# A decoder layer on one core: one of the feed-forward operands is split again from its fp32 rows instead of being stored as two halves

## The chip, the cores and the metric

One of the eight cores of a Trainium2 chip runs the whole layer as one program. The metric is the device time of one execution in microseconds (us); lower is better. The engines are named as the profile names them: PE is TensorE, ACT is ScalarE, DVE is VectorE, POOL is GpSimd, SP is SyncE.

## What is computed

The reference is one hybrid decoder layer on a sequence of 2048 rows of 1024 fp32 values (`h`), with DEPTH 1:

```
u   = h @ W_in                                   # q | k | v | rnn-x | rnn-gate
att = sliding_window_sink_attention(q, k, v)     # 8 heads of 64, window 128
rec = rg_lru(causal_dwconv(rnn-x)) * gelu(rnn-gate)
mix = concat(att, rec) @ W_out
h   = LN1(alpha*h + mix)
ffn = (gelu(causal_dwconv(gate)) * val) @ w_down     with  gate | val = h @ w_up
ple = sigmoid(h @ W_g + b_g) * (p @ W_p)
h   = LN2(alpha*h + ffn + ple)
```

All matrix products are wanted to nearly fp32 accuracy.

## The kernel before

**Three products for one.** Each fp32 operand is split into two values that TensorE takes in one pass: a high half (ACT copies the fp32 tile to the type fp32r, line 122) and a low half (DVE subtracts the high half from the fp32 tile, line 123). This is `split_sb`. A product is then three matmuls, high by high, high by low, low by high (`mm3`, lines 140 to 142). So every weight block that SP loads (`wraw`, L132, into one of three `wst` buffers) passes through ACT and DVE before PE can take it.

**The first half of the layer, four chunks.** A loop `c` = 0 to 3 goes over chunks of 512 rows. In each it does the input projection, the recurrent branch, attention, the output projection and LN1, and then transposes the normalised rows with PE (L567). ACT and DVE make three things of each transposed tile: the halves `hh_[u]` and `hl_[u]` that the gate of the per-layer embedding needs at once, and the unsplit fp32 copy `hf[u]`. The index `u` = 0 or 1 names the first or the second 512 of the 1024 features. POOL then stores to DRAM what the feed-forward part will need: `hf[0]` and `hf[1]` (L573), and some of the split halves (L576). Behind these stores in POOL's queue, or ahead of them, stand the two loads of the next chunk's input (`xs`, L325). After that the chunk does the embedding's projection (`pps`, L596 copies its PSUM result out) and its gate (`gated`), each in two column halves `dh`. For `dh` = 1 the weights are loaded anew by SP.

**The second half, two pairs of chunks.** The feed-forward product `h @ w_up` is done for two chunks at a time (`s2` = 0 for chunks 0 and 1, `s2` = 1 for 2 and 3) with Strassen's seven products for eight. The operand's four quarters are B11 (features half 0, first chunk of the pair), B12 (half 0, second chunk), B21 (half 1, first chunk) and B22 (half 1, second chunk). B11, B21 and B22 are also used unsummed, in products of their own; the sums are T1 = B12 - B11, T3 = B22 - B12, T2 = T3 + B11 and T4 = B21 - T2. Before, the split halves of B11, B21 and B22 go to DRAM in the first half (`hxd`) and come back as they are (`load_split`, L258 and L261). The sums are made in `combine` from the fp32 rows that `stage` fetches with POOL (L239): for each of four k-tiles `kt`, B11 and B12 go into the two buffers of the ring `xb`, B22 into `xd`, B21 into `pch` or `pcl`. `combine` makes the sums on DVE (L279, L280, L282, L285) and splits T1 to T3 with `operand`, one ACT cast and one DVE subtract each. For pair 0 this runs while chunk 3's gate is computed, for pair 1 while the down-projection of chunk 1 runs.

**What sets the order.** The tile framework's scheduler orders the instructions of each engine when the program is built, by program order and by what it thinks is ready; each engine and each DMA queue then runs its list in order. PE's list is fixed by hand in `up` alone. The big tiles (operands, halves, `hf`, `xs`) share 13 slots of one ring, `h`; a tile waits there for the last reader of the slot's tile before it, a storing DMA included.

Of the kernel before, what the change touches and what calls it, by code (L numbers as in the profile page):

```python
# [8 lines left out]
F32 = mybir.dt.float32  # L9
# [6 lines left out]
P = 128  # L16
T = 512
# [17 lines left out]
def f(ap):  # L35
    return ap.bitcast(F32)
# [3 lines left out]
def kernel(  # L40
# [13 lines left out]
    ACT, DVE, POOL, PE, SP = nc.scalar, nc.vector, nc.gpsimd, nc.tensor, nc.sync  # L54
# [27 lines left out]
    def tm(tag, dt=F32, cols=512):  # L82
        return tmp.tile([P, cols], dt, tag=tag, name=nm(tag), bufs=BUFS.get(tag, 2))

    def h8(name, shape, dt=F32R):

        return h_p.tile(shape, dt, tag="h", name=nm(name))
# [15 lines left out]
    def order(i, earlier):  # L103
        for e in earlier:
            tc.add_manual_dep(
                i.ins, e.ins.name,
                mybir.DependencyInfo(mybir.DependencyClass.NoSync, mybir.DependencyReason.DATA),
                reason="issue order")
        return i
# [11 lines left out]
    def split_sb(src, hi, lo, eng=None):  # L121
        ACT.copy(hi, src)  # L122
        (eng or DVE).tensor_tensor(lo, src, f(hi), ALU.subtract)  # L123
# [73 lines left out]
    def scratch(name, shape, dt):  # L197
        return dr.tile(shape, dt, tag=name, name=name)

    rsd = [scratch(f"rsd{i}", [P, DM], F32) for i in range(NCH * NTOK)]  # L200
    hfd = [[scratch(f"hf{c}_{u}", [P, 4, T], F32) for u in range(2)] for c in range(NCH)]
    hxd = [{n: [scratch(f"hx{n}_{s}_{m}", [P, 4, T], F32) for m in range(2)] for n in ("B11", "B21", "B22")}
           for s in range(2)]
    gd = [[scratch(f"gd{s}_{k}", [P, 4, 2 * T], F32) for k in range(NF // 4)] for s in range(2)]

# [30 lines left out]
    hx = [{}, {}]  # L236
# [5 lines left out]
    def operands(s2, names):  # L242
        for n in names:
            hx[s2][n] = [[t[:, k, :] for k in range(4)] for t in (h8(n, [P, 4, T]), h8(n, [P, 4, T]))]

    def operand(s2, n, kt, src):
        split_sb(src, hx[s2][n][0][kt], hx[s2][n][1][kt])
# [3 lines left out]
    def load_split(s2, n, earlier):  # L251

        hx[s2][n] = []
        for m in range(2):
            if (n, m) == ("B22", 1):
                ts = [tm(("pch", "pcl")[k % 2], F32R) for k in range(4)]
                for k in range(4):
                    order(POOL.dma_start(f(ts[k]), hxd[s2][n][m][:, k, :]), earlier)  # L258
            else:
                t = h8(n, [P, 4, T])  # L260
                order(POOL.dma_start(f(t), hxd[s2][n][m]), earlier)  # L261
                ts = [t[:, k, :] for k in range(4)]
            hx[s2][n].append(ts)
# [8 lines left out]
    def combine(s2, kt):  # L272

        if kt == 0:
            load_split(s2, "B11", ())
            operands(s2, ("T2", "T1", "T3"))
        b11, b12, b22, b21 = staged[kt]
        t3, t1, t2 = (tm("xc") for _ in range(3))
        DVE.tensor_tensor(t3, b22, b12, ALU.subtract)  # L279
        DVE.tensor_tensor(t2, t3, b11, ALU.add)  # L280
        operand(s2, "T2", kt, t2)
        DVE.tensor_tensor(t1, b12, b11, ALU.subtract)  # L282
        operand(s2, "T1", kt, t1)
        operand(s2, "T3", kt, t3)
        DVE.tensor_tensor(b21, b21, t2, ALU.subtract)  # L285
# [6 lines left out]
    for c in range(NCH):  # L292

        def t_pair(name):
            return [[h8(name + m, [P, 4, T]) for _ in range(2)] for m in "hl"]
# [117 lines left out]
        for j in range(4):  # L413
            a, s, xc = rts[j][:, 0, :], rts[j][:, 1, :], xcs[j]
# [144 lines left out]
        hh_, hl_ = t_pair("h")  # L559
# [11 lines left out]

        for u in range(2):
            POOL.dma_start(hfd[c][u], hf[u])  # L573
        for u in range(c % 2, 2):
            for m, t in enumerate((hh_[u], hl_[u])):
                POOL.dma_start(hxd[c // 2][("B11", "B21", None, "B22")[2 * (c % 2) + u]][m], f(t))  # L576


        fence()
# [6 lines left out]
        for dh in range(2):  # L586
# [12 lines left out]
            for t_ in range(NTOK):  # L599
                ts_ = slice(t_ * P, (t_ + 1) * P)  # L600
                acc = bank("acc")
                for k in range(8):
                    b = ws[k // 2][k % 2]
                    gated = mm3(acc, hh_[k // 4][:, k % 4, ts_], hl_[k // 4][:, k % 4, ts_],
                        b[:, 0, :], b[:, 1, :], k == 0, k == 7)
                sg = tm("P")
                DVE.tensor_tensor(sg, acc, bg[:, ds_], ALU.add)
                act(sg, sg, AF.Sigmoid)
                DVE.tensor_tensor(sg, sg, pps[t_], ALU.mult)
                d = rs[t_][:, ds_]  # L610
                DVE.scalar_tensor_tensor(d, d, ALPHA, sg, ALU.mult, ALU.add)
                if dh == 1:
                    POOL.dma_start(rsd[c * NTOK + t_], rs[t_])
                if c == NCH - 1:
                    i = 4 * dh + t_
                    if i % 2 == 0:
                        stage(0, i // 2, last_scores)
                    else:
                        combine(0, i // 2)
# [108 lines left out]
    def down(s2):  # L728
# [5 lines left out]
        for ch in range(2):  # L734
# [32 lines left out]
            for kp in range(NF // 2 - 2):  # L767
                for dh in range(2):
                    wb = wunit(W_DOWN + 12 * dh + kp)
                    for t_ in range(NTOK):  # L770
                        i = sums(kp, t_, dh, gb, wb)
                    if dh == 0:
                        marks.append(i)
                gb = gated_pair(kp + 1)
                if later:
                    later.pop(0)()
                if c == 1 and 2 < kp < 7:
                    stage(1, kp - 3, marks[-1:])
                if c == 1 and 3 < kp < 8:
                    combine(1, kp - 4)  # L780
                if kp == NF // 4:
                    for t_ in range(NTOK):
                        rt = tm("r", cols=DM)
                        POOL.dma_start(rt, rsd[c * NTOK + t_])
                        rs.append(rt)
# [101 lines left out]
```

## Time and profile before

| | us |
|---|---|
| median of 3 runs | 2334.41 |
| lowest and highest of them | 2331.52 and 2335.72 |
| the profiled execution's own time | 2334.86 |
| its span, first to last instruction | 2333.2 |
| outside the span | 1.66 |

The profile is of one execution. A group line gives line, engine, operation and tiles, then count, busy time and mean duration. A line of a timeline gives start and duration in us, engine, line, operation and tiles and, in brackets, how long the engine sat idle before it and who released it. Matmuls are pipelined, so the distance between two starts, not the duration shown, is what one costs. In views by window the column PEclk is the granted TensorE clock as a share of full speed, and the DMA columns are the mean busy share of the 16 DMA engines and the GB/s that they moved.

### The profile page before, as it was taken

How to read it: one execution, taken by the hardware profiler on the slowest of the kernel's cores; microseconds unless marked ns; L12 is line 12 of the kernel's file. 1: busy time of each engine (PE TensorE's matmuls, PEld its weight loads, DVE VectorE, ACT ScalarE, POOL GpSimd, SP SyncE). 2: the span in 40 equal slices, each digit the busy share in tenths (PEclk: the TensorE clock that was granted, in tenths of full speed). 3: DMA queues.
4: the chain of work that ended last, by engine and by line, in shares of the span. 5: the costliest groups of instructions: out<-in, count | busy, mean ns of one | idle time of the engine just before them, and what ended most of it. 6: DMA issues, size and time to landing. Idle time of an engine off the chain costs nothing.

```text
span 2333.2 us, 28422 instructions
## 1 busy us (share of the span) xinstructions
PE 2279.2 (98%) x10156; PEld 1865.8 (80%) x10156; DVE 1654.2 (71%) x2728; ACT 1089.5 (47%) x2034; POOL 254.6 (11%) x477
## 2 busy tenths in 40 slices
PE   9998999999999999999999999999999999999998
PEld 7777877877787777888888888888888888888887
DVE  7975797678668888777777743768777777753735
ACT  7644674466456564444444433344544444433321
POOL 0311140013002311100000000010000000000000
PEclk9999999999999999999999999999999999999999
DMA  5336424532633465222222354664322222254642
GB/s 164 100 96 239 142 66 161 209 109 79 236 131 105 145 234 185 83 85 89 83 82 82 127 180 153 253 207 167 110 87 89 82 82 82 82 203 149 215 148 79
DMA packets 94638, 314.93 MB, mean 135 GB/s; under 512 B 9888, under 2 KB 10016, under 8 KB 89888
## 3 DMA queue, kind: packets, MB, share of 16 engines
q1 hardware_dynamic: 79200, 239.70, 31.1%
q0 software_dynamic: 15296, 73.41, 8.4%
q8 instruction: 80, 1.31, 0.2%
q14 instruction: 62, 0.51, 0.1%
HBM read 250.16 MB, written 62.91 MB: 134 GB/s over the span
## 4 chain that ended last, share of the span: by engine, by line
PE 59%; DVE 1%; DMA 0%; issue 0%; POOL 0%; DVEq 0%; POOLq 0%
PE b L140 7%; PE b L142 7%; PE b L141 7%; PE acc L142 5%; PE a L142 5%; PE a L140 5%; PE acc L140 5%; PE a L141 5%; PE acc L141 5%; PE sc L142 2%; PE sc L140 2%; PE sc L141 2%; DMA wst<-in_w_dram 0%; DVE st L214 0%; DVE r L798 0%; DVE r L220 0%
## 5 line engine op out<-in xcount | busy, mean ns | idle before, releaser
L122 ACT CAST wb<-wst 128x512 fp32r<-128x512 f32 x640 | 393.0, 622 | 672.9 <-PE acc L142 326.3
L123 DVE TENSOR_TENSOR wb<-wst,wb 128x512 fp32r<-128x512 f32 x640 | 434.2, 685 | 271.9 <-ACT wb L122 271.3
L140 PE MATMUL b<-T,wb 128*128 128x512 f32 x576 | 224.6, 390 | 1.6 <-DVE xd L686 0.8
L142 PE MATMUL b<-T,wb 128*128 128x512 f32 x576 | 224.1, 389 | 0.0
L141 PE MATMUL b<-T,wb 128*128 128x512 f32 x576 | 224.1, 389 | 0.0
L122 ACT CAST wb<-xc 128x512 fp32r<-128x512 f32 x144 | 89.3, 620 | 190.6 <-PE a L142 92.5
L141 PE MATMUL a<-B,wb 128*128 128x512 f32 x384 | 149.5, 389 | 0.1
L140 PE MATMUL a<-B,wb 128*128 128x512 f32 x384 | 149.4, 389 | 0.0
L142 PE MATMUL a<-B,wb 128*128 128x512 f32 x384 | 149.4, 389 | 0.0
L123 DVE TENSOR_TENSOR wb<-xc,wb 128x512 fp32r<-128x512 f32 x144 | 98.9, 687 | 49.2 <-ACT wb L122 49.2
L140 PEld LDWEIGHTS b<-T,wb 128*128 128x128 f32 x576 | 108.1, 188 | 25.7 <-DVE xd L686 1.9
L142 PEld LDWEIGHTS b<-T,wb 128*128 128x128 f32 x576 | 108.1, 188 | 22.5
L141 PEld LDWEIGHTS b<-T,wb 128*128 128x128 f32 x576 | 108.1, 188 | 22.4
L639 DVE SCALAR_TENSOR_TENSOR pl<-xb,prm,pl 128x512 f32<-128x512 f32 x96 | 71.8, 748 | 76.4 <-POOL xb L702 73.9
L142 PE MATMUL acc<-wb,hl 128*128 128x512 f32 x256 | 100.6, 393 | 1.7 <-DVE hl L98 1.7
L140 PE MATMUL a<-xh,wb 128*128 128x512 f32 x256 | 101.8, 398 | 0.0
L141 PE MATMUL a<-xl,wb 128*128 128x512 f32 x256 | 101.4, 396 | 0.0
L142 PE MATMUL a<-xh,wb 128*128 128x512 f32 x256 | 101.4, 396 | 0.0
L141 PE MATMUL acc<-wb,hh 128*128 128x512 f32 x256 | 100.5, 393 | 0.1
L140 PE MATMUL acc<-wb,hh 128*128 128x512 f32 x256 | 99.2, 393 | 1.0 <-ACT hh L97 1.0
L141 PEld LDWEIGHTS a<-B,wb 128*128 128x128 f32 x384 | 72.1, 188 | 15.5 <-DMA B<-hxB 0.5
L142 PEld LDWEIGHTS a<-B,wb 128*128 128x128 f32 x384 | 72.1, 188 | 14.9
(277 smaller groups left out, 5719.1 us busy)
## 6 DMA issues: line engine op xcount, KB each, us to landing
wst<-in_w_dram SPq DMA_DIRECT2D x319, 512.0 KB, 3.6
graw<-gd SPq DMA_DIRECT2D x24, 1024.0 KB, 6.4
gd<-pl SPq DMA_DIRECT2D x48, 256.0 KB, 2.0
gd<-r SPq DMA_DIRECT2D x48, 256.0 KB, 4.2
B<-hxB POOLq DMA_DIRECT2D x10, 1024.0 KB, 8.7
r<-in_xn_dram SPq DMA_DIRECT2D x16, 512.0 KB, 4.1
ln<-in_rows_dram POOLq DMA_DIRECT2D x16, 512.0 KB, 4.9
hf<-hf POOLq DMA_DIRECT2D x8, 1024.0 KB, 8.0
```

What stands on the lines that cost most here:

```text
L122: ACT.copy(hi, src)
L123: (eng or DVE).tensor_tensor(lo, src, f(hi), ALU.subtract)
L140: order(PE.matmul(o, ah, bh, start=first, stop=False, skip_group_check=more), after)
L141: PE.matmul(o, ah, bl, start=False, stop=False, skip_group_check=more)
L142: return PE.matmul(o, al, bh, start=False, stop=last, skip_group_check=more)
L639: DVE.scalar_tensor_tensor(gc, xb[:, t_:t_ + T], pc(C_FW + 3 * ft + t_), gc, ALU.mult, ALU.add)
```

## The change

The DRAM copies of B11's halves are gone, and with them their stores in chunks 0 and 2 (two of 1 MiB each per chunk) and their loads at the first step of `combine` (two of 1 MiB per pair). In their place `combine` treats B11 as it treats the sums: two tiles of the same ring `h` are taken by `operands`, and in each of its four steps `operand` splits the fp32 tile `b11`, which is fetched for the sums anyway. Per pair these are four ACT casts and four DVE subtracts of 128x512. The halves come out with the same values, because `hf` is the same PSUM tile that the stored halves were made from.

```diff
-    hxd = [{n: [scratch(f"hx{n}_{s}_{m}", [P, 4, T], F32) for m in range(2)] for n in ("B11", "B21", "B22")}
+    hxd = [{n: [scratch(f"hx{n}_{s}_{m}", [P, 4, T], F32) for m in range(2)] for n in ("B21", "B22")}
            for s in range(2)]
@@ def combine(s2, kt):
         if kt == 0:
-            load_split(s2, "B11", ())
-            operands(s2, ("T2", "T1", "T3"))
+            operands(s2, ("B11", "T2", "T1", "T3"))
         b11, b12, b22, b21 = staged[kt]
         t3, t1, t2 = (tm("xc") for _ in range(3))
         DVE.tensor_tensor(t3, b22, b12, ALU.subtract)
+        operand(s2, "B11", kt, b11)
         DVE.tensor_tensor(t2, t3, b11, ALU.add)
@@ for c in range(NCH):
         for u in range(2):
             POOL.dma_start(hfd[c][u], hf[u])
-        for u in range(c % 2, 2):
-            for m, t in enumerate((hh_[u], hl_[u])):
-                POOL.dma_start(hxd[c // 2][("B11", "B21", None, "B22")[2 * (c % 2) + u]][m], f(t))
+        for m, t in enumerate((hh_[1], hl_[1])):
+            POOL.dma_start(hxd[c // 2][("B21", "B22")[c % 2]][m], f(t))
```

## Rows read from the trace of the kernel before

**Rows 1.** The page, part 1: busy time, share of the span, instructions.
```profile
PE 2279.2 (98%) x10156; PEld 1865.8 (80%) x10156; DVE 1654.2 (71%) x2728; ACT 1089.5 (47%) x2034; POOL 254.6 (11%) x477
```

**Rows 2.** PE's waits, whole span: who released it, total us, times, longest.
```profile
PE a L140 <- ACT ph L596: 12.5, 3, 6.1
```

**Rows 3.** PE's timeline at the embedding's second half, chunk 0, then chunk 2.
```profile
197.70 0.39 PE L140 MATMUL a<-wb,pt 128*128 128x512 f32 x1
...
200.19 0.39 PE L142 MATMUL a<-wb,pt 128*128 128x512 f32 x1
206.64 0.80 PE L140 MATMUL a<-wb,pt 128*128 128x512 f32 x1 [6.06 <-ACT ph L596]
...
211.39 0.40 PE L142 MATMUL a<-wb,pt 128*128 128x512 f32 x1
...
636.83 0.39 PE L142 MATMUL a<-wb,pt 128*128 128x512 f32 x1
...
648.32 0.40 PE L142 MATMUL acc<-wb,hl 128*128 128x512 f32 x1
```

**Rows 4.** PE's timeline at the same place in chunk 1, then in chunk 3.
```profile
423.02 0.39 PE L142 MATMUL a<-wb,pt 128*128 128x512 f32 x1
423.46 0.50 PE L140 MATMUL a<-wb,pt 128*128 128x512 f32 x1
...
858.62 0.39 PE L142 MATMUL a<-wb,pt 128*128 128x512 f32 x1
860.38 0.50 PE L140 MATMUL a<-wb,pt 128*128 128x512 f32 x1 [1.38 <-ACT ph L596]
```

**Rows 5.** Windows of 1 us: PE, PEld, DVE, ACT, POOL busy, PEclk, DMA, GB/s.
```profile
201.00:202.00 1.00, 0.00 (x0) 0.00 (x0) 0.00 (x0) 0.00 (x0) 0.00 (x0) 1.00 1.00 414
...
206.00:207.00 1.00, 0.36 (x1) 0.36 (x2) 0.86 (x2) 1.00 (x3) 0.00 (x0) 0.50 0.29 119
...
419.00:420.00 1.00, 1.00 (x6) 0.84 (x5) 1.00 (x3) 0.93 (x2) 0.00 (x0) 1.00 0.54 49
```

**Rows 6.** ACT's timeline, chunk 0, just before PE goes on.
```profile
205.49 0.62 ACT L122 CAST wb<-wst 128x512 fp32r<-128x512 f32 x1 [6.07 <-DMA wst<-in_w_dram]
```

**Rows 7.** DMA issues from 195 to 196, then 418 to 419: us to landing last.
```profile
wst<-in_w_dram SPq DMA_DIRECT2D x1, 512.0 KB, 9.3
...
wst<-in_w_dram SPq DMA_DIRECT2D x1, 512.0 KB, 3.6
```

**Rows 8.** POOL's timeline: issue of stores and loads, chunk 0, then chunk 1.
```profile
177.66 0.54 POOL L576 DMA_DIRECT2D hxB<-hh  x1 [4.76 <-ACT hh L97]
...
183.45 0.53 POOL L325 DMA_DIRECT2D xs<-in_xt_dram  x1
...
395.75 0.53 POOL L325 DMA_DIRECT2D xs<-in_xt_dram  x1
402.22 0.54 POOL L573 DMA_DIRECT2D hf<-hf  x1 [5.94 <-ACT hf L570]
```

**Rows 9.** Tile T: count, duration in ns (least, median, most), first and last start.
```profile
L122 ACT CAST T<-xc x24: 615/619/716, 834.9 to 1551.8; 128x512 fp32r<-128x512 f32 x24
L123 DVE TENSOR_TENSOR T<-xc,T x24: 680/684/694, 836.7 to 1552.6; 128x512 fp32r<-128x512 f32 x24
```

**Rows 10.** Windows of the two stretches of combine, pair 0 and pair 1.
```profile
845.00:885.00 40.00, 38.62 (x170) 31.64 (x169) 34.21 (x56) 20.43 (x37) 5.54 (x12) 1.00 0.57 205
...
1500.00:1560.00 60.00, 60.00 (x266) 49.67 (x266) 38.74 (x62) 25.65 (x46) 7.57 (x15) 1.00 0.72 254
```

**Rows 11.** Timelines of DVE and PE, pair 0; last, us to landing of tile hf.
```profile
849.37 0.69 DVE L123 TENSOR_TENSOR T<-xc,T 128x512 fp32r<-128x512 f32 x1 [1.71 <-DMA hf<-hf]
...
872.82 0.68 DVE L123 TENSOR_TENSOR T<-xc,T 128x512 fp32r<-128x512 f32 x1
...
885.01 0.39 PE L140 MATMUL a<-B,wb 128*128 128x512 f32 x1
...
DMA to landing us min/median/max: 3.3/4.5/9.5
```

## The prediction

> **What bounds the kernel now.** I read the busy times first. PE is busy 2279.2 us of a span of 2333.2 us, so all that any edit off PE can win is in the 54 us in which PE is idle, plus what PE does at half clock [rows 1]. Next I read PE's waits. The largest entry is not a wait for data that PE multiplies: PE waits for ACT to copy the embedding's projection out of PSUM (L596), three times, 12.5 us together [rows 2]. The timeline shows where: at the second column half of the embedding, in chunk 0 (6.06 us), in chunk 2 and in chunk 3 (1.38 us) [rows 3, 4]; what is left of 12.5 for chunk 2 is about 5.1. At the same place in chunk 1 PE hardly pauses [rows 4]. That contrast is the key to the case, because chunks 0 and 2 are just those that store four split halves through POOL, and chunks 1 and 3 store two.
>
> Why PE waits there is read backwards. ACT's list in front of the copy holds the cast of a weight block, and that cast sat idle 6.07 us for the weight's DMA [rows 6]. This weight had been issued between 195 and 196 and took 9.3 us to land; its twin in chunk 1 took 3.6 [rows 7]. The windows show why: at 201 all 16 DMA engines are fully busy at 414 GB/s, and the load has fallen off only in the window from 206; in chunk 1 it has fallen to 49 GB/s by 419, about when the twin is issued [rows 5]. So the weight comes late in chunks 0 and 2 because POOL's stores and the next chunk's input fill the DMA engines.
>
> **What a pause costs.** In chunk 0 the matmuls before the pause start 0.226 us apart: 11 steps from 197.70 to 200.19 [rows 3]. Twelve steps from 200.19 to 211.39 take 11.20 us instead of 12 x 0.226 = 2.72, a loss of 8.48. The 2.4 us above the wait itself are the clock: it is at 1.00 at 201 and at 0.50 (1.2 GHz) when PE resumes at 206.64 [rows 5]. In chunk 2, 15 steps from 636.83 to 648.32 take 11.49 instead of 3.40, a loss of 8.09 [rows 3]. In chunk 1 the same step takes 0.44, a loss of 0.21; in chunk 3 it takes 1.76, a loss of 1.53, hardly more than the wait, so the clock was kept there [rows 4].
>
> **The change part by part.**
>
> *Two stores fewer in chunks 0 and 2.* This is 2 x 1024 KB = 2.10 MB per chunk, at 414 GB/s 5.07 us of all DMA engines [rows 5]. The traffic of chunks 0 and 2 then equals that of chunk 1: two stores of `hf`, two of halves, two input loads, the same weights. I take chunk 1 as the model: the losses become 0.21 each. Gain: (8.48 - 0.21) + (8.09 - 0.21) = 16.15 us. It also needs chunk 1's order. There the first input load goes out at 395.75, ahead of the stores, while POOL waits for `hf` till 402.22; in chunk 0 POOL stands instead in front of the store of `hh_[0]` and the input load comes last, at 183.45 [rows 8]. With that store gone the scheduler has in chunk 0 the list that it had in chunk 1, so I expect the same order. If the input load stays last, the DMA backlog still ends 5.07 us sooner: a wait of 6.06 - 5.07 = 1.0 us in chunk 0, about 0 in chunk 2, and by chunk 3's example no fall of the clock. The gain is then (8.48 - 1.15) + (8.09 - 0.15) = 15.3, under 1 us less. The gain is not given back later: PE is busy nearly all the time after these places and runs its list in order.
>
> *Two loads fewer per pair.* They are 2.10 MB in stretches where DMA is busy 57% and 72% [rows 10]. Nobody on PE's path is seen waiting for them; I cost them at nothing, and below nothing in the bounds.
>
> *Four casts and four subtracts more per pair.* One cast is 0.619 us, one subtract 0.684 [rows 9], so 2.48 us of ACT and 2.74 us of DVE per pair. For pair 1 PE is busy 60.00 of 60 us while DVE is busy 38.74 and ACT 25.65 [rows 10]: 21 us of idle DVE hide it, cost 0. For pair 0 DVE is busy 34.21 of 40 us [rows 10], and PE has its one small wait there, 1.38 us at 860.38, behind DVE's sum for the gate in ACT's list. What hides the new work is a hole of 1.71 us on DVE before 849.37, where it waits for a slot that a store of `hf` still reads, and the time between the last split at 872.82 + 0.68 = 873.5 and the first product on B11 at 885.01, 11.5 us [rows 11]. The new wait is DVE's for ACT's cast: behind it stand the sums, the gate's additions and the weight splits of the same queue, and PE waits for those. Bounds: below, chunk 3's loss of 1.53 goes entirely, since fewer bytes move; above, all eight new instructions of pair 0 in series on PE's path, 2.48 + 2.74 = 5.2 us. I take 0: the hole and the slack together exceed the 2.74, and the fetched row is there already.
>
> *Slots and POOL.* B11's two tiles take two slots of the ring `h` as before, only written by ACT and DVE. The halves of features half 0 lose a reader. POOL issues eight DMAs less, 0.53 to 0.54 us each [rows 8], on an engine that is busy 11% [rows 1]: nothing.
>
> *Sum.* 2334.86 (the profiled execution, 2333.2 of it span) - 16.15 + 0 = 2318.7. That execution is 0.45 above the median of the three runs, so I say 2318.5. The bounds of pair 0 make it 2317 to 2324.
>
> **The rivals.**
>
> *The weight is not helped by a shorter queue.* In chunk 0 the weight landed at about 195.8 + 9.3 = 205.1, just as the backlog ended [rows 5, 7]; I read this as the weight sharing badly until the others are through. If instead it gets a fixed share for as long as others are active, its 9.3 us depend on the backlog's presence, not its length. With the input load still last, the backlog of 2.10 MB less would end near 201, 5 us after the issue. The weight would be as late as now: 2334.9, no change. For it speaks only that the order may stay. Against it: 512 KB at half of 414 GB/s is 2.5 us, well short of the 5.7 us that 9.3 lies above 3.6; and in chunk 1's order the question does not arise. The Trainium skill (DMA: Bandwidth & Descriptors, Queues, rings and completion order) states such a rule: each DMA engine takes turns packet by packet between the queues that have work. By that rule the time could stay at 2334.9; the 9.3 us of this trace speak for a worse share than one turn in two.
>
> *Only one of the two pauses goes,* because the scheduler deals the two chunks differently. Against it: the two look alike now in loss (8.48 and 8.09). Time: 2334.9 - 8.1 = 2326.8.
>
> *Pair 0's sums come too late.* The place is the start of `up` for pair 0. `b11` has two readers more, its ring `xb` has two buffers and a step takes both, so the next step's fetches can go out only after the split; and POOL's queue, with the `hf` and gate stores of chunk 3 behind the fetch, stands meanwhile. The four steps now take from 834.9, where the first T is cast [rows 9], to 873.5, 9.65 us each. If each also waited for the slowest fetch, 9.5 us [rows 11], and for its own cast and subtract, 1.3, a step would take 20.5 and the last split would end near 834.9 + 82 = 917. PE, which wants it at 885, would stand 32 us, and 2.4 more for the clock: 2318.7 + 34 = 2353. It decides the sign only if the split ends some 30 us later than today's 873.5: 11.5 of slack, then 16.15 + 4.7 - 2.4 = 18.4 us of pause. Against it: the last reader of `b11` is the sum T1 in any case, behind the place of the new split, and the median fetch is 4.5 us [rows 11].
>
> *The change does not do what it says*, for instance because the input loads fill the time that the stores leave: that ends where the first rival does.
>
> **How the numbers follow.** The forecast, with either order of the input load, has a chance of 0.77: 2318.5. One pause of two: 0.09, 2327. No gain: 0.08, 2335. Too late: 0.06, slower. What this kernel's measurement can tell from no change is about 0.2%, 4.7 us. So faster 0.86, same 0.08, slower 0.06. The forecast alone leaves out 0.23, so the range reaches to the case of one pause: from 2315 (the lower bound of pair 0 and the scatter of the runs, 2 us) to 2327.
>
> **What would show it.** Right: PE's wait for L596 falls from 12.5 us to under 3; the granted clock stays at 1.00 through chunks 0 and 2; the weight issued near 196 lands in about 4 us; POOL's first input load in chunk 0 stands ahead of the stores of `hf`; T's 24 casts get eight like them on B11. Wrong: a pause of over 3 us at that place still, with DMA at 414 GB/s through it; or a new wait of PE for ACT or DVE between 840 and 900. The prediction fails if the scheduler, whose order I infer from chunk 1, deals chunk 0 in another way, or if pair 0's DVE queue, 86% busy, passes its delay on to PE.

## The result, and the profile after

| | before | after |
|---|---|---|
| median (lowest to highest), us, 4 runs each | 2334.73 (2331.52 to 2335.72) | 2320.67 (2320.08 to 2321.56) |
| the profiled execution, us | 2334.86 | 2321.56 |
| its span, us | 2333.2 | 2319.9 |

The ratio is 0.9942, with a 95% interval of 0.9925 to 0.996. The same two kernels on another chip gave 0.9945 (0.9932 to 0.9959, medians 2323.73 and 2336.14; last experiment). The changed kernel is thus 0.4 to 0.75% faster, 12 to 14 us by the medians.

First the page of the kernel after, part 1, against [rows 1]:

```profile
PE 2274.1 (98%) x10156; PEld 1863.4 (80%) x10156; DVE 1657.9 (71%) x2736; ACT 1092.3 (47%) x2042; POOL 259.9 (11%) x469
```

PE does the same 10156 matmuls. DVE and ACT have eight instructions more, the splits of B11, and POOL has eight fewer. The next rows are the waits of PE in the kernel after, to be held against [rows 2] (line 596 is now 595), and then the casts of B11:

```profile
PE a L140 <- ACT ph L595: 3.3, 3, 1.4
PE b L140 <- DVE ph L669: 2.0, 2, 1.6
PE a L141 <- DMA B<-hxB: 1.0, 1, 1.0
...
L122 ACT CAST B<-xb x8: 614/622/653, 817.0 to 1533.9; 128x512 fp32r<-128x512 f32 x8
```

The wait that the prediction is about has fallen from 12.5 us to 3.3. Two small ones, 1.6 and 1.0 us, are at the start of the feed-forward of pair 0. Here is PE's timeline at the old pauses, chunk 0 and chunk 2, against [rows 3]:

```profile
197.43 0.39 PE L142 MATMUL a<-wb,pt 128*128 128x512 f32 x1
199.05 0.50 PE L140 MATMUL a<-wb,pt 128*128 128x512 f32 x1 [1.23 <-ACT ph L595]
...
201.70 0.39 PE L142 MATMUL a<-wb,pt 128*128 128x512 f32 x1
...
627.83 0.39 PE L142 MATMUL a<-wb,pt 128*128 128x512 f32 x1
628.92 0.50 PE L140 MATMUL a<-wb,pt 128*128 128x512 f32 x1 [0.71 <-ACT ph L595]
...
632.23 0.39 PE L142 MATMUL acc<-wb,hl 128*128 128x512 f32 x1
```

The twelve steps from 197.43 to 201.70 take 4.27 us instead of 2.72, a loss of 1.55 where before had 8.48. The 15 steps from 627.83 to 632.23 take 4.40 instead of 3.40, a loss of 1.00 where before had 8.09. Gained: 6.93 and 7.09 us. Next POOL's timeline in chunk 0, the issue of the weight (us to landing last), and two windows of 1 us (PE, PEld, DVE, ACT, POOL busy, PEclk, DMA, GB/s); they answer to [rows 5, 7, 8]:

```profile
170.20 0.53 POOL L325 DMA_DIRECT2D xs<-in_xt_dram  x1
176.65 0.54 POOL L573 DMA_DIRECT2D hf<-hf  x1 [5.93 <-ACT hf L570]
...
wst<-in_w_dram SPq DMA_DIRECT2D x1, 512.0 KB, 4.8
...
193.00:194.00 1.00, 1.00 (x6) 0.84 (x5) 1.00 (x2) 0.92 (x3) 0.00 (x0) 1.00 0.12 45
...
199.00:200.00 1.00, 0.95 (x4) 0.82 (x5) 1.00 (x3) 1.00 (x3) 0.00 (x0) 1.00 0.77 287
```

The input load went ahead of the stores, as in chunk 1 of before. By 193, when the weight was issued, the DMA engines were down to a busy share of 0.12: the backlog was nearly through (17 packets of POOL's queue were still to come, and the second input load landed at 196.14). The weight took 4.8 us instead of 9.3, and the clock stayed at 1.00.

**Where the 13.3 us of span came from.** I set the start of each matmul of after against the same matmul of before.

| stretch | gained, us |
|---|---|
| start of the run, up to 183 us | +2.7 |
| pause of chunk 0 | +7.0 |
| pause of chunk 2 | +7.0 |
| start of attention in chunks 2 and 3 | -2.6 |
| end of chunk 3 and start of pair 0's feed-forward | -1.1 |
| later | -0.7 |
| small steps | +1.0 |

The first row lies ahead of the places that the change touches. Some 1.9 us of it come in the first 15 us; the other 0.8 come at chunk 0's attention near 80 us, where both kernels are at a granted clock of 0.50 and before is back at 1.00 some matmuls later. PE's timeline shows the larger part, first of before, then of after:

```profile
12.35 0.63 PE L141 MATMUL acc<-xl,wb 128*128 128x512 f32 x1
12.77 0.63 PE L142 MATMUL acc<-xh,wb 128*128 128x512 f32 x1
13.20 0.43 PE L140 MATMUL acc<-xh,wb 128*128 128x512 f32 x1
```

```profile
9.18 0.74 PE L141 MATMUL acc<-xl,wb 128*128 128x512 f32 x1
9.76 0.39 PE L142 MATMUL acc<-xh,wb 128*128 128x512 f32 x1
9.98 0.39 PE L140 MATMUL acc<-xh,wb 128*128 128x512 f32 x1
```

Matmuls start 0.43 us apart until 13.20 in one and until 9.76 in the other, then 0.23 apart. In a second profile of the changed kernel the pace rose later again, and by 15 us its matmuls were 3.1 us behind those of the first. So spans of single profiles differ by up to 3 us for this alone, and I compare places, not whole spans. The losses at attention are stretches at a granted clock of 0.50 (505 to 508 and 720 to 723 in after, 1.00 at the same matmuls in before). The experiments below have the same attention code: pair 1's split alone kept its clock in chunk 2 and lost it in chunk 3 (725), while the two that keep all the pauses of before, stores back and input load first, lost it in both (near 512 and 734). So the loss doesn't go with the change; I put it down to scatter. That the +2.7 and the -2.6 nearly cancel in this pair of profiles is luck.

### The profile page after: what moved, and what is told of

It reads as the page before. It is cut to its first block, busy times and chain, and to the rows that moved or that the text cites. A ratio compares the mean times of both kernels' runs of the same rounds, so it can differ in the third digit from the quotient of the medians.

```text
span 2319.9 us, 28423 instructions
## 1 busy us (share of the span) xinstructions
PE 2274.1 (98%) x10156; PEld 1863.4 (80%) x10156; DVE 1657.9 (71%) x2736; ACT 1092.3 (47%) x2042; POOL 259.9 (11%) x469
## 4 chain that ended last, share of the span: by engine, by line
PE 59%; DVE 2%; DMA 0%; issue 0%; ACT 0%; POOL 0%; DVEq 0%; POOLq 0%
PE b L140 7%; PE b L141 7%; PE b L142 7%; PE a L141 5%; PE a L140 5%; PE a L142 5%; PE acc L140 5%; PE acc L141 5%; PE acc L142 5%; PE sc L141 2%; PE sc L142 2%; PE sc L140 2%; DMA wst<-in_w_dram 0%; DVE st L214 0%; DVE r L797 0%
```

## The experiments

Each ratio is against runs of before on the same chip. Stores back, stores late, input load last and input load first shared one chip and 19 runs of before (median 2335.05); pair 0 alone, pair 1 alone, the stores in chunk 1 and the copies first in the changed kernel another (27 runs, 2334.63); one store, the copies first with late stores, no split and the change again a third (9 runs, 2336.14). The diffs show the lines that matter: declarations, and the lists (`hf_out`, `halves_out`, `copies`) in which the instructions to be ordered behind are collected, are left out.

**Stores back, split kept.**

```diff
-        for m, t in enumerate((hh_[1], hl_[1])):
-            POOL.dma_start(hxd[c // 2][("B21", "B22")[c % 2]][m], f(t))
+        for u in range(c % 2, 2):
+            for m, t in enumerate((hh_[u], hl_[u])):
+                POOL.dma_start(hxd[c // 2][("B11", "B21", None, "B22")[2 * (c % 2) + u]][m], f(t))
```

> The changed kernel with B11's four stores put back in chunks 0 and 2 and never read; B11 is still split from its rows. Theory D (the POOL stores hold the DMA engines until after the gate's weight is issued): PE's wait for the copy of the embedding's projection comes back, about 6 us in chunk 0 and 5 in chunk 2, with the clock at 0.5 behind it; 2320.7 + 7.1 + 6.8 = 2334.6. Rival L (the loads that fell away, or the new split, made the difference): it stays at 2321.

Measured: 2336.78, ratio 1.0005 (0.9996 to 1.0014). Waits of PE in this kernel:

```profile
PE a L140 <- ACT ph L596: 12.2, 3, 5.7
PE b L140 <- DVE ph L670: 2.4, 2, 2.0
```

With the stores back the whole gain is gone, and the wait is back at 12.2 us. The missing loads and the split together bring nothing without the missing stores.

**Stores kept, but issued late.** The kernel before, with B11's two stores taken out of the loop that stores the halves and put behind the chunk's gate; loads and products as before.

```diff
+        if c % 2 == 0:
+            for m, t in enumerate((hh_[0], hl_[0])):
+                order(POOL.dma_start(hxd[c // 2]["B11"][m], f(t)), [gated])
```

> The kernel before with B11's stores kept and read as before, but issued behind the gate of chunks 0 and 2. Same bytes in all, none of B11's in the critical stretch, no split from rows. Theory D: waits of about 1 us, 2334.7 - 14 = 2320.7, and up to 1 us less, as pair 0 has no new work. Rival L: 2334.7.

Measured: 2323.52 (2322.08 to 2325.53), ratio 0.9953 (0.9936 to 0.9969). Chunk 0 on PE:

```profile
200.95 0.50 PE L140 MATMUL a<-wb,pt 128*128 128x512 f32 x1 [1.09 <-ACT ph L595]
```

POOL issued the two stores at 225.03 and 225.55 instead of 177.66 and after. No byte was saved and no split added, and the pause is as short as in after. What counts is that the 2.10 MB aren't ahead of the weights, not that they are gone. The input load went first here too (172.16), but the order alone is worth nothing, as the experiment after the next shows. These experiments together name the cause.

**Input load last.** The changed kernel, with the next chunk's input ordered behind the stores of the halves, as it stood in chunk 0 of before.

```diff
-                order(POOL.dma_start(st, xt[c, :, 4 * u:4 * u + 4, :]), have_h)
+                order(POOL.dma_start(st, xt[c, :, 4 * u:4 * u + 4, :]), have_h + halves_out)
```

> The changed kernel with the next chunk's first input load put behind the stores of the halves, in chunks 0 to 2. Fewer bytes, old order. Theory D: the backlog is as short as in the changed kernel but starts later, by up to some 5 us: waits of about 1 to 2 us in each of the chunks 0 to 2, no fall of the clock, 2321 to 2325. Rival S (a weight load is as late as long as any backlog is there): 6, 6 and 5 us with the fall of the clock, 2340. Rival O (only the order counts): 2334 or more.

Measured: 2322.93 (2321.6 to 2324.31), ratio 0.9947 (0.9933 to 0.9962). The waits for the projection's copies are 1.3 and 0.6 us in all:

```profile
200.31 0.62 ACT L122 CAST wb<-wst 128x512 fp32r<-128x512 f32 x1 [1.25 <-DMA wst<-in_w_dram]
...
201.47 0.50 PE L140 MATMUL a<-wb,pt 128*128 128x512 f32 x1 [0.59 <-ACT pl L596]
```

The weight was issued at 194.70 and took 5.5 us; the two input loads ahead of it landed at 196.03 and 198.62. A shorter backlog helps though a backlog is still there when the weight is issued. So the rival by which only its presence counts falls.

**Input load first, all bytes kept.** The kernel before, with the stores of halves ordered behind those of `hf`; POOL then issues the input load at 172.01, ahead of the stores.

```diff
-                POOL.dma_start(hxd[c // 2][("B11", "B21", None, "B22")[2 * (c % 2) + u]][m], f(t))
+                order(POOL.dma_start(hxd[c // 2][("B11", "B21", None, "B22")[2 * (c % 2) + u]][m], f(t)), hf_out)
```

> The kernel before with the order of the changed one: in chunks 0 and 2 the store of the first half of h stands behind the stores of the fp32 copy, so the next chunk's first input load goes out first. All bytes as before. Theory D: the input load uses the time in which the DMA engines were 0.6 to 0.7 busy, worth 2 to 3 us; waits of 3 to 4 us in chunks 0 and 2, 2334.7 - 6 = 2328 to 2332. Rival O: waits of about 1, 2321. Nothing gained: 2334.7.

Measured: 2335.8 (2333.16 to 2338.08), ratio 1.0002 (0.9993 to 1.0012). The pause in chunk 0 is still there, and the awaited weight, issued at 194.86, takes 10.1 us:

```profile
wst<-in_w_dram SPq DMA_DIRECT2D x1, 512.0 KB, 10.1
...
206.25 0.80 PE L140 MATMUL a<-wb,pt 128*128 128x512 f32 x1 [6.58 <-ACT ph L597]
```

I had expected a part of the gain from the order; there is none.

**The change for pair 0 alone, and for pair 1 alone.** Each keeps the kernel before for the other pair. The diff is that of pair 0; for pair 1 the 1 of `s2 == 1` is a 0 and the 2 of `c == 2` a 0.

```diff
-            operands(s2, ("B11", "T2", "T1", "T3"))
+            if s2 == 1:
+                load_split(s2, "B11", ())
+                operands(s2, ("T2", "T1", "T3"))
+            else:
+                operands(s2, ("B11", "T2", "T1", "T3"))
...
+        for u in range(0 if c == 2 else 1, 2):
+            for m, t in enumerate((hh_[u], hl_[u])):
+                POOL.dma_start(hxd[c // 2][("B11", "B21", None, "B22")[2 * (c % 2) + u]][m], f(t))
```

> The change for pair 0 alone: chunk 0 has two stores of halves and pair 0 splits B11 from its rows; chunk 2 still stores B11's halves and pair 1 loads them. Theory (each pause belongs to the four stores of its own chunk; pair 0's new split costs about 1 to 1.5 us, pair 1's nothing): PE's wait for the projection's copy is about 1 us in chunk 0 and about 5 us in chunk 2; time about 2320.7 + 6.8 = 2327.5. Rival (the two pauses hang together, for instance by a schedule that is dealt anew for all chunks): both go or both stay, 2321 or 2335.

> The change for pair 1 alone: chunk 2 has two stores of halves, chunk 0 four, pair 0 loads B11's halves as the kernel before does. Theory: chunk 0's pause of about 6 us stays, chunk 2's falls to about 1 us, and pair 0's extra 1 to 1.5 us are not paid; time about 2320.7 + 7.1 - 1.2 = 2326.6. If pair 0's split costs nothing, as I had put it, 2327.8. Rival (the pauses hang together): 2321 or 2335.

Measured: 2328.6 (2326.85 to 2330.49), ratio 0.9976 (0.9967 to 0.9985), and 2329.29 (2326.63 to 2330.87), 0.9974 (0.9965 to 0.9983). PE's waits at the place, first pair 0 alone (its pause is in chunk 2), then pair 1 alone (in chunk 0):

```profile
634.40 0.58 PE L140 MATMUL a<-wb,pt 128*128 128x512 f32 x1 [4.70 <-ACT ph L601]
```

```profile
205.68 0.80 PE L140 MATMUL a<-wb,pt 128*128 128x512 f32 x1 [6.57 <-ACT ph L601]
```

Each pause belongs to its own chunk: 6.0 us are won by the one and 5.3 by the other, 11.4 together, beside 12 to 14 for the whole change. That pair 1 alone would be the faster for want of pair 0's split did not show in the medians.

**Two stores more in chunk 1.** The changed kernel, in which chunk 1 now stores four halves.

```diff
+        for u in range(0 if c == 1 else 1, 2):
+            for m, t in enumerate((hh_[u], hl_[u])):
+                POOL.dma_start(hxd[c // 2][("B11", ("B21", "B22")[c % 2])[u]][m], f(t))
```

> The changed kernel with two stores more in chunk 1, the halves of features half 0, which nobody reads; so chunk 1 now has the four stores that chunks 0 and 2 have lost. Theory (bytes ahead of the weight load make the pause, whichever chunk it is): a wait of PE of about 5 to 6 us appears in chunk 1 at the embedding's second half, with the clock at 0.50 behind it, and its weight takes about 9 us instead of 3.6; time about 2320.7 + 7.5 = 2328. Rival (something else of chunks 0 and 2, such as their place in a pair, makes the pause): no pause in chunk 1, 2321.

Measured: 2328.62 (2326.85 to 2331.88), ratio 0.9975 (0.9966 to 0.9985). The three weights (the line gives their median; the first, which is awaited, took 8.2 us), PE in chunk 1, and the windows from there:

```profile
wst<-in_w_dram SPq DMA_DIRECT2D x3, 512.0 KB, 8.6
...
417.67 0.50 PE L140 MATMUL a<-wb,pt 128*128 128x512 f32 x1 [4.60 <-ACT ph L596]
...
417.00:418.00 1.00, 0.33 (x1) 0.30 (x2) 0.84 (x2) 1.00 (x3) 0.00 (x0) 1.00 0.98 401
...
419.00:420.00 1.00, 1.00 (x4) 0.71 (x4) 0.46 (x2) 0.57 (x1) 0.00 (x0) 0.50 0.11 45
```

Where there was no pause, one of 4.60 us appears, followed by the half clock, and the time is what was expected to within 1 us. The cause can be put into a chunk and taken out of it.

**One store of the two.** The changed kernel with `hh_[0]` alone stored in chunks 0 and 2.

```diff
+        if c % 2 == 0:
+            POOL.dma_start(hxd[c // 2]["B11"][0], f(hh_[0]))
```

> The changed kernel with one of the two removed stores back in chunks 0 and 2 (the high halves of features half 0, 1 MiB, read by nobody). Theory (the weight lands when the bytes ahead of it are through): 1.05 MB at 414 GB/s is 2.5 us, so the waits for the projection's copy are about 3.7 us in chunk 0 and 3.2 in chunk 2 and the weight takes about 7 us; with or without the clock's fall 2320.7 + 5 to 9 = 2326 to 2330. Rival (a threshold: the weight is late only if the store of hh_[0] stands first in POOL's list and so puts the input load last): as long as with both stores, 2335; or (one store is hidden) 2321.

Measured: 2325.43 (2323.68 to 2327.44), ratio 0.9958 (0.9944 to 0.9971), a little under the expected span of 2326 to 2330. The first awaited weight took 8.0 us in chunk 0. PE there, and a window behind it:

```profile
204.21 0.50 PE L140 MATMUL a<-wb,pt 128*128 128x512 f32 x1 [2.67 <-ACT pl L597]
...
206.00:207.00 1.00, 1.00 (x4) 0.81 (x3) 1.00 (x2) 1.00 (x4) 0.00 (x0) 0.50 0.46 49
```

PE's waits there are 2.67 us in chunk 0 and 1.4 in chunk 2, below the 3.7 and 3.2 of the theory, partly because here the first copy stood ahead of the late cast in ACT's list. Between none and two stores lies a middle; it's no all-or-nothing. In time the interval overlaps that of the changed kernel on the same chip, so the middle rests on the trace.

**The copies first in ACT's list.** The changed kernel, in which the casts of the third and fourth weight of `dh` = 1 are ordered behind the first two copies of L595 (`copies`); then the same edit on the kernel with late stores.

```diff
-            ws = [wunit(W_PG + 4 * dh + u) for u in range(4)]
+            ws = [wunit(W_PG + 4 * dh + u, copies[:2] if dh == 1 and u >= 2 else ()) for u in range(4)]
```

> The changed kernel with the copies of the projection's first two results (second column half) put ahead of the casts of the third and fourth weight in ACT's list, in all chunks; nothing else is changed. Theory (what is left of the pauses is ACT standing in front of a weight's cast while the copy that PE wants stands behind it): PE's waits for the projection's copy, now 3.3 us in three places, fall to under 1, a gain of 2 to 3.5 us, so about 2318. Rival (PE wants the late weight anyway a moment later): the wait moves from the copy to the weight's halves, and the time stays within 1 us of 2320.7.

> The kernel before with two edits: B11's stores issued only behind the chunk's gate, so that they are no longer ahead of the weights and B11 is still loaded as halves; and the projection's first two copies put ahead of the casts of the third and fourth weight. Theory: the pauses go as in the changed kernel, the 2 to 3 us that are left of them go too, and pair 0 pays for no split, so nothing is given back there: 2320.7 - 2.5 - 1.1 = 2317. Rival (a later point, attention or the feed-forward's start, holds the end in any case): within 1 us of 2320.7.

Measured: 2319.75 (2315.3 to 2322.22), ratio 0.9937 (0.9924 to 0.9949), and 2321.26 (2317.4 to 2322.38), ratio 0.9937 (0.9924 to 0.9949). PE's waits between 825 and 925 us, first of the one with the split, then of the one with late stores:

```profile
PE b L140 <- DVE ph L669: 3.4, 1, 3.4
PE a L140 <- ACT ph L595: 0.6, 1, 0.6
```

```profile
PE b L140 <- DVE xd L688: 1.4, 1, 1.4
PE b L140 <- DVE ph L672: 1.2, 1, 1.2
```

The waits for the copies fall to 0.6 us and to none that is listed. Against the changed kernel, matmul by matmul, PE in the kernel with the split wins 1.5, 0.2, 1.0 and 0.8 us at this place in chunks 0 to 3 (nothing is left of the loss in the first three), and gives 1.8 and more back at pair 0's start, where its wait for DVE grows from 1.6 to 3.4. With late stores it wins 1.5, 0.2, 1.0 and 1.3 and gives back nothing there. Both are faster than the kernel before; neither is shown to be faster than the changed one, since the intervals overlap.

**The split by itself, and the change again.**

```diff
-            operands(s2, ("B11", "T2", "T1", "T3"))
+            operands(s2, ("T2", "T1", "T3"))
+            hx[s2]["B11"] = hx[s2]["T2"]
...
-        operand(s2, "B11", kt, b11)
```

> The changed kernel without B11's split: B11's two tiles, four casts and four subtracts per pair are gone, and T2's tiles are multiplied in B11's place, so B11's own product is not computed; stores and loads are those of the changed kernel. It measures the split by itself. Theory (pair 0's split costs about 1 to 1.5 us, because DVE stands behind the last cast, which waits for its fetched row; pair 1's nothing): PE's waits near the start of the feed-forward of pair 0, now 1.6 us for DVE and 1.0 us for B11's halves, shrink by about 1 us in all; about 2319.6. Rival (the split is hidden, as I had put it at 0, and what is lost there is the order of the other work): the waits stay and the time is 2320.7.

> The changed kernel itself, unaltered, beside the three others on one chip, so that differences of a few us between them can be read: 2320.7 by its earlier runs.

Measured: 2319.51 (2318.5 to 2320.85) without the split, ratio 0.9933 (0.992 to 0.9945), and 2323.73 (2320.47 to 2326.55) for the change. PE's waits from 825 to 925 us, without the split and with it:

```profile
PE b L140 <- DVE xd L685: 1.2, 1, 1.2
PE b L140 <- DVE ph L669: 1.2, 1, 1.2
```

```profile
PE b L140 <- DVE ph L669: 2.3, 1, 2.3
PE a L140 <- ACT ph L595: 1.3, 1, 1.3
```

The waits go from 3.6 us (4.0 in the first profile of after) to 2.4. I added up the same waits (behind the projection, the sums and B11's halves) in all profiles: the eight with a split in pair 0 have 3.2 to 5.1 us, 4.0 on average, the six without, the kernel before among them, 2.4 to 3.7, 3.0 on average. That puts the split at about 1 us, but the sets overlap, and the late-store kernel has 3.7 without any split, so the scheduler's dealing of the same work moves as much. One of these waits parts the two sets: that for DVE's `ph` (L669 here) is 1.6 to 3.4 us in the eight and 0.6 to 1.2 in the six. The difference of the medians, 4.2 us, is more than the waits explain, and the intervals of the two ratios overlap.

The repeat taught something else. Chunk 0 on PE in the repeat, and the windows:

```profile
202.76 0.79 PE L140 MATMUL a<-wb,pt 128*128 128x512 f32 x1 [2.52 <-ACT ph L595]
...
202.00:203.00 1.00, 0.24 (x1) 0.24 (x2) 0.74 (x2) 1.00 (x3) 0.00 (x0) 0.87 0.63 254
203.00:204.00 1.00, 1.00 (x3) 0.81 (x4) 1.00 (x2) 1.00 (x3) 0.00 (x0) 0.50 0.03 12
```

The same program waited 2.52 us here and lost its clock, where the first profile waited 1.23 and kept it. Its first weight took 6.1 us against 4.8, with as few packets of POOL's queue behind the issue (18 against 17), so what is left of the backlog doesn't explain the difference. What is left of the pause is not a fixed sum: by the count of steps the loss in chunk 0 is 4.4 us here and 1.55 there.

## Why the prediction was right, and where its terms were off

The forecast was 2318.5 us; 2320.67 came, inside the range. Step by step:

- **The cause.** Right, and shown from both sides: stores back without the other parts, 1.0005; stores moved in time with nothing else changed, 0.9953; stores put into chunk 1, a new pause there. The chain from the late weight to the cast, the copy and PE stood as read.
- **The order of the input load.** Right that the scheduler would deal chunk 0 like chunk 1, and right that it matters little: 2320.67 and 2322.93 with the load first and last have overlapping intervals (0.9942 and 0.9947). The prediction's "under 1 us less" isn't contradicted: the ratios are 0.0005 apart, 1.2 us, which is within the scatter. The order without the bytes is worth nothing (1.0002).
- **Chunk 1 as the model.** Mis-sized. I took its loss of 0.21 for chunks 0 and 2; it is 1.55 and 1.00. The first weight took 4.8 us in chunk 0, where chunk 1's had 3.6 [rows 7], so the cast behind which the copy stands is still late. That step promised 16.15 us; by the same count of matmuls 6.93 + 7.09 = 14.02 came. Putting the copy ahead of the cast takes the rest away in chunks 0 to 2, which shows where it sits; why the weight needs 1.2 us more than in chunk 1, and 2.5 more in the repeat, with the backlog nearly gone stays open.
- **Pair 0's split at 0.** Mis-sized, by about 1 us as far as the waits tell, inside my bounds of -1.53 to 5.2. The cover that I named, the hole and the 11.5 us of slack on DVE, was spent elsewhere: POOL issues the last step's fetch behind a cast on ACT (before, DVE's sum T1 released it, after 3.08 us), ACT's cast of B11 waits for the fetched row, and DVE for that cast. POOL, ACT and DVE of after:

```profile
850.15 1.06 POOL L239 DMA_DIRECT2D xb<-hf  x2 [4.97 <-ACT T L122]
...
854.95 0.62 ACT L122 CAST B<-xb 128x512 fp32r<-128x512 f32 x1 [4.49 <-DMA xb<-hf]
...
855.60 0.69 DVE L123 TENSOR_TENSOR B<-xb,B 128x512 fp32r<-128x512 f32 x1 [2.96 <-ACT B L122]
```

  This is the mechanism of my third rival at a thirtieth of its price: DVE stands 2.96 us, has next to no idle time after it, and a result of its list that PE wants at 878.2 (`ph`) comes at 879.7. My 32 us took every fetch at its slowest and no overlap between the four steps.
- **Pair 1 at 0.** Right: PE has no wait between 1490 and 1560 in after.
- **The signs.** Input load first, eight casts on B11, the clock at 1.00 at both old pauses: as said. The wait came to 3.3 us instead of under 3 and the weight to 4.8 instead of about 4, which is the mis-sized term above. Of the signs of being wrong one came in small: PE's wait for DVE at 879.77, 0.6 us in before, is 1.6.
- **No gain, because the weight has a fixed share.** Wrong in its outcome: with the input load last a backlog was still there, and the pause fell to 0.59 us. Its mechanism is partly in the trace. The queues of before in chunk 0, after the weight's issue at 195.76 (q0 is POOL's, q1 SP's: packets, MB, share of 16 engines), from 196 to 198, from 198 to 200, from 200 to 202:

```profile
q0 software_dynamic: 106, 0.75, 101.0%
...
q0 software_dynamic: 95, 0.69, 86.9%
q1 hardware_dynamic: 22, 0.09, 15.2%
...
q0 software_dynamic: 70, 0.52, 62.3%
q1 hardware_dynamic: 64, 0.26, 32.7%
```

  SP's queue moves nothing in the first 2 us and 22 packets in the next two; only from 200 on is it served nearly packet for packet, 64 to 70. Some of this is a load's own start: the weight that chunk 1 issued between 418 and 419 had its first packets in the window from 419. The three weights issued from 195.76 to 199.37 share what SP's queue gets: it had moved 1.13 MB when the first of them, 0.52 MB, had landed. POOL's packets are also nearly twice as large (0.52 MB in 70, 0.26 MB in 64), so an even count still leaves SP's queue a third of the engines' time, 32.7%. The Trainium skill (DMA: Bandwidth & Descriptors, Queues, rings and completion order) says that an engine takes turns between its queues packet by packet. The counts from 200 on are as that would have them and those from 198 to 200, 95 to 22, are not; but the page means by a packet a group of descriptors, and no run shows that the profile's packets of 4 and 8 KB are those. So my "sharing badly until the others are through" was right for the first 4 us and too strong for the rest.

## What to carry to other kernels

When PE waits for a small copy, walk back through the list of the copying engine to the load that holds it up, and look at who fills the DMA engines when that load is issued: there, issuing 2 MB of stores at 225 us instead of 177 was worth nearly as much as never storing them. A cast that waits for a late load should not stand in front of a result that PE already wants. And a gain at one pause is only kept if nothing behind it is bound to another engine: the 3.5 us won by reordering ACT were partly eaten at the next place where PE follows DVE.

## What the runs showed that I had not expected

The same program twice differed by 5.0 us of span (2319.9 and 2324.9): 3.1 us in the first 15 us of the run, where matmuls start 0.43 us apart for 3 to 6 us longer or shorter, and most of the rest at one pause with its clock. Behind the pauses of 2.52, 2.67, 4.60 and 6.06 us the granted clock went to 0.50; behind those of 1.23 and 1.38 it stayed at 1.00. In between both occur: behind 1.90 us in chunk 3, with the stores in chunk 1, it fell; behind 2.04 us at pair 0's start, with the stores back, it stayed. So a pause can be paid for twice, and one and the same pause isn't paid alike in each execution.

The transfers' place in a queue was worth nothing as long as the bytes were the same: with the first input load 11 us earlier (172.01 instead of 183.45) the awaited weight still took 10.1 us and PE still stood 6.58.
